# Gated scores and the state's part of the output as 64-row matmuls in the two halves of the array, both groups side by side

## The chip, the cores and the metric

The kernel runs on one core of a Trainium2 chip. TensorE multiplies matrices: a stationary operand is loaded into its array of 128 rows by 128 columns (a weight load, "PEld" in the profile), a moving operand streams past it (a matmul, "PE"), and the result goes to PSUM, eight banks of 512 fp32 numbers on each of 128 partitions. VectorE (DVE), ScalarE (ACT) and GpSimd (POOL) work element by element; SyncE (SP) issues most transfers. The metric is the device time of one execution in microseconds.

## What is computed

One decoder layer over 1024 rows of width 1024, in fp32. The part that the change touches is the gated linear attention: four heads, keys of 64, values of 128.

```python
b = jnp.cumsum(log_a, axis=-2)
qe = q * jnp.exp(b)
ke = k * jnp.exp(-b)
A = jnp.where(causal, jnp.einsum('bhncd,bhnsd->bhncs', qe, ke), 0.0)
o_intra = jnp.einsum('bhncs,bhnsv->bhncv', A, v)
# state of a chunk: S * decay + kd^T v, carried from chunk to chunk
o_inter = jnp.einsum('bhncd,bhndv->bhncv', qe, S_prev)
o = o_intra + o_inter
```

The output goes through a normalisation per head and a SiLU gate. Beside it runs a sliding-window softmax attention of eight query heads, then an output projection, and a convolutional gated MLP of width 2816, which takes most of the time.

## The kernel before

The 1024 rows are eight tiles (t = 0 to 7) of 128 rows. A dense unit multiplies one tile with one block of a weight matrix: eight steps over the depth, each in three passes of reduced-precision fp32 products (`dense`, line 317). The GLA phase takes the place of two 64-row chunks of the reference by one of 128 rows.

For each tile of the GLA:

- `unit_g` projects queries and keys (tile `dg`), and `gla_qk` multiplies them by the exponentials of the cumulated gate into `qe` and `kd`.
- `gla_tr` transposes both on TensorE into the bank `gt` (L560): four blocks, two for the queries and two for the keys. A block holds a pair of heads, the even head on partitions 0 to 63, the odd one on 64 to 127. ScalarE copies the keys into one tile (`gkt`, L565) and the queries into `qbd` (L563), a block-diagonal tile: for each pair two blocks of 128 columns, the first with the even head's rows and zeros below, the second with zeros above and the odd head's rows. The zeros are written once at the start (L517).
- `gla_a` (L591) multiplies, for each pair, all 128 key rows with the 256 columns of `qbd`. The zeros keep the two heads apart. The scores of four heads land in one bank `ga`; `copy_predicated` (L593) writes those on and below the diagonal into `asb`, which was zeroed at the start.
- `gla_o` adds up in one bank `go` the product of masked scores and values for each head (L600) and, from the second tile on, the product of the block of `qbd` with the state `s_mid` (L603). ScalarE squares the result (L606), VectorE sums the squares (L608) and copies the result over the values (L609).
- `gla_state` (L573, bank `cs`) makes the tile's contribution to the state, in two halves of 64 columns of the array; `gla_mid` (L586) and VectorE (L581) carry the state on in the two `s_mid` tiles in turn.

All of these products are of plain fp32 operands. `swa_pv` (L490, banks `pv`) of the window attention already uses array halves: first two column halves, then four quarters of 64 rows by 64 columns. A written order chains its matmuls.

The work is put down as a list of events with due times (`at(time, function, ...)`), sorted by time. Dense unit t of the queries and keys stands at TG + t; of tile t, `gla_tr` stands 1.0 later, `gla_mid` and `gla_state` at 1.75 and 1.8, `gla_a` at 1.9, `gla_o` at 2.7. A planner then orders each engine's instructions by its own model, and takes whatever is ready; only chained instructions keep their order. Transposes, decay products (`dec`, L538), cumulated gates (`bd`, L530) and the window attention's scores (`sc`), transposes (`ppt`) and outputs (`pv`) lie between the dense units.

Banks come from two pools of four in turn (`bank`): each request takes the bank that was given out eight requests earlier, once its readers are done. Small tiles of 2 KB a partition rotate through `K2` buffers (`k2_tile`).

Of the kernel before, what the change touches and what calls it, by code (L numbers as in the profile page):

```python
# [9 lines left out]
F32 = mybir.dt.float32  # L10
F32R = mybir.dt.float32r
I32 = mybir.dt.int32
AF = mybir.ActivationFunctionType
# [4 lines left out]
P = 128  # L18
# [12 lines left out]
HALF = (slice(0, 64), slice(64, 128))  # L31
# [3 lines left out]
def hymba_layer_kernel(ctx, tc, x, mix_norm, w_in, w_alpha2, b_alpha, gla_norm,  # L35
                       q_norm, k_norm, sinks, w_out, ffn_norm, w_up, conv_w,
                       conv_b, w_down, out):
    nc = tc.nc
    act, dve, pool, pe, sp = nc.scalar, nc.vector, nc.gpsimd, nc.tensor, nc.sync
# [15 lines left out]
    def bank(name):  # L55
        ps["n"] += 1
        if "f" in ps:
            return ps["f"][2 + ps["n"] % 2]

        for start, which in (("n2pt_6", "b"), ("do1_7", "a"), ("n2pt_3", "a")):  # L60
            if name.startswith(start):
                return ps[which].tile([P, 512], F32, tag="b", name=name)
        return ps["ab"[ps["n"] % 2]].tile([P, 512], F32, tag="b", name=name)

    big = base.tile([P, NT, KD, 2, P], F32R, name="big")

    RAW_BUFS, K4, K2, N_WARM = 3, 6, 5, 5

    def raw_tile(name):
        return base.tile([P, 1024], F32, tag="raw", name=name, bufs=RAW_BUFS)  # L70
# [33 lines left out]
    gl = sg.enter_context(tc.tile_pool(name="gl", bufs=1))  # L104
# [11 lines left out]
    amask = upper.bitcast(I32)  # L116
# [45 lines left out]
    def rms_scale(ss, n, w, name, p, tag, bufs=3):  # L162
        v = p.tile([P, w], F32, tag=tag + "v", name=name + "v", bufs=bufs)
        dve.tensor_scalar(v, ss, 1.0 / n, EPS, op0=ALU.mult, op1=ALU.add)
        r = p.tile([P, w], F32, tag=tag + "r", name=name + "r", bufs=bufs)
        pool.tensor_tensor(r, v, mhalf[:, :w], ALU.pow)
        return r
# [156 lines left out]
    kt = gl.tile([P, 2, T + P], F32R, name="kt")  # L324
# [24 lines left out]
    def k2_tile(name):  # L349
        return gl.tile([P, 512], F32, tag="k2", name=name, bufs=K2)  # L350
# [119 lines left out]
    def swa_pt(t, g):  # L470
# [10 lines left out]
            dve.tensor_sub(pt[:, 0], pb, pt[:, 1])  # L481
        pts[t, g] = pt

    def swa_pv(t):

        pbs = [bank(f"pv{t}_{i}")[:, 0:256].rearrange("p (j c) -> p j c", j=4) for i in range(2)]

        def part(g, b, rows, i, start, stop):
            rhs = pts[t, g][:, b, :].rearrange("p (j c) -> p j c", j=4)
            pe.matmul(pbs[i][HALF[g]], lhsT=vv[rows, t - 1 + b, HALF[g]], rhs=rhs[rows, :, HALF[i]],  # L490
                      start=start, stop=stop)
            ins = nc.cur_bb.bb.instructions[-1]
            if order:
                tc.add_manual_dep(ins, order[-1], mybir.DependencyInfo(
                    mybir.DependencyClass.NoSync, mybir.DependencyReason.DATA), reason="order of the program")
            order.append(ins.name)

        full, order = slice(0, P), []
        for i in range(2):
            for g in (1, 0):  # L500
                part(g, i if t else 1, full, i, True, t == 0)


        if t:
            for g in (1, 0):
                for i in range(2):
                    part(g, 1 - i, HALF[i], i, False, True)
        for i in range(2):
            act.copy(qo[:, t, :].rearrange("p (j c) -> p j c", j=4)[:, :, HALF[i]], pbs[i])
# [1 line left out]


    s_mid = [gl.tile([P, 2, P], F32, name=f"s_mid{i}") for i in range(2)]
    qbd = [gl.tile([P, 2, 2, P], F32, name=f"qbd{i}") for i in range(2)]
    asb = gl.tile([P, 4, P], F32, name="asb")
    for s in qbd + [asb]:
        pool.memset(s, 0.0)  # L517
    gkd, gdec, gfac, gex, gqk, gqt, glh, grs, vg = {}, {}, {}, {}, {}, {}, {}, {}, [None]

    def gla_lh(t):  # L520
        lh = k2_tile(f"lh{t}").bitcast(F32R).rearrange("p (r c) -> p r c", r=2)
# [34 lines left out]
    def gla_tr(t):  # L556
        pb = bank(f"gt{t}")
        for i in range(4):
            src = (gqk, gkd)[i // 2][t]
            pe.transpose(pb[:, i * P:(i + 1) * P], src[:, i % 2 * P:(i % 2 + 1) * P], ident)  # L560
        pv = pb.rearrange("p (i c) -> p i c", i=4)
        for lo in range(2):
            act.copy(qbd[t % 2][HALF[lo], :, lo, :], pv[HALF[lo], 0:2])  # L563
        kt = k2_tile(f"gkt{t}")[:, 0:256].rearrange("p (i c) -> p i c", i=2)
        act.copy(kt, pv[:, 2:4])  # L565
        gqt[t] = kt

    def gla_state(t):
        kd, v, fc, sm = gkd[t], vg[0][:, t, :], gfac[t + 1], s_mid[(t + 1) % 2]
# [14 lines left out]
    def gla_mid(t):  # L584
        for pr in range(2):
            act.activation(s_mid[t % 2][:, pr], s_mid[(t - 1) % 2][:, pr], AF.Copy, scale=gfac[t][:, pr:pr + 1])  # L586

    def gla_a(t):
        pb = bank(f"ga{t}")
        for pr in range(2):  # L590
            pe.matmul(pb[:, pr * 256:(pr + 1) * 256], lhsT=gqt[t][:, pr, :], rhs=qbd[t % 2][:, pr],  # L591
                      start=(pr == 0), stop=(pr == 1))
        dve.copy_predicated(asb, amask.rearrange("p (q c) -> p q c", q=1).broadcast_to((P, 4, P)),  # L593
                            pb.rearrange("p (q c) -> p q c", q=4))

    def gla_o(t):
        v = vg[0][:, t, :]
        pb = bank(f"go{t}")
        for h in range(4):
            pe.matmul(pb[:, h * P:(h + 1) * P], lhsT=asb[:, h, :], rhs=v[:, h * P:(h + 1) * P],  # L600
                      start=(h == 0), stop=(t == 0 and h == 3))
        for h in range(4 if t else 0):
            pe.matmul(pb[:, h * P:(h + 1) * P], lhsT=qbd[t % 2][:, h // 2, h % 2, :], rhs=s_mid[t % 2][:, h // 2, :],  # L603
                      start=False, stop=(h == 3))
        sq = k2_tile(f"gsq{t}")
        act.activation(sq, pb, AF.Square)  # L606
        ss = gl.tile([P, 4], F32, tag="gss", name=f"gss{t}", bufs=2)
        dve.tensor_reduce(ss, sq.rearrange("p (h d) -> p h d", d=P), op=ALU.add, axis=AX.X)  # L608
        dve.tensor_copy(v, pb)  # L609
        grs[t] = rms_scale(ss, P, 4, f"g{t}", gl, "gr", 8)  # L610

    def gate(t, pb):
# [7 lines left out]
    def gate_tr(t, gs):  # L620
        pb = bank(f"ogt{t}")
        for h in range(4):
            pe.transpose(pb[:, h * P:(h + 1) * P], gs[:, h * P:(h + 1) * P], ident)
        pv = pb.rearrange("p (h c) -> p h c", h=4)
        hi, lo = big[:, t, 0:4, 0, :], big[:, t, 0:4, 1, :]
        act.activation(hi, pv, AF.Copy, scale=glan)
        dve.scalar_tensor_tensor(lo, pv, glan, hi.bitcast(F32), op0=ALU.mult, op1=ALU.subtract)
        src = qo[:, t, :].rearrange("p (j c) -> p j c", j=4)
        hi, lo = big[:, t, 4:8, 0, :], big[:, t, 4:8, 1, :]
        split(src, hi, lo)  # L630
# [422 lines left out]
    def at(time, f, *a):  # L1053
        ev.append((time, len(ev), f, a))
# [34 lines left out]
    for c in halves:  # L1089
        split(mix_row[:, c], mix_hl[0][0:1, c], mix_hl[1][0:1, c], dve)  # L1090
        pb = bank(f"mix{len(mix_ps)}")
# [77 lines left out]
    for t in range(NT):  # L1169
        s = 11.0 + 1.9 * t  # L1170
        at(s - 0.3, swa_qt, t)
        at(s + 1.0, swa_scores, t, 0)
        at(s + 1.6, swa_scores, t, 1)
        at(s + 3.2, swa_pt, t, 0)
        at(s + 3.8, swa_pt, t, 1)
        at(s + 4.9, swa_pv, t)
        s = TG + t
        at(s - 2.4, gla_lh, t)
        at(s - 1.4, gla_exp, t)
        at(s + 1.0, gla_tr, t)  # L1180
        if t < NT - 1:
            if t:
                at(s + 1.75, gla_mid, t + 1)
            at(s + 1.8, gla_state, t)
        at(s + 1.9, gla_a, t)
        at(s + 2.7, gla_o, t)
        at(TR + t + 1.3, lambda tt=t: gate_tr(tt, psb.pop(("r", tt))))
    at(TO + 8.006, mark)
    at(TO - 0.05, open_acc)
# [9 lines left out]
    for n, (ch, name) in enumerate(LOW):  # L1199
# [6 lines left out]
    order = [(ch, i, name) for ch in range(NCH)  # L1206
             for i, name in enumerate({0: SEQ_FIRST, L: SEQ_LAST}.get(ch, SEQ)) if (ch, name) not in LOW]
# [96 lines left out]
```

## Time and profile before

| | |
|---|---|
| Time, median of 3 runs | 1055.09 us (1054.99 to 1056.57) |
| Profiled execution | 1055.06 us |
| Its span, first to last instruction | 1053.3 us |
| TensorE busy | 1046.6 us (99%) |
| VectorE, GpSimd, ScalarE busy | 801.7, 617.4, 480.2 us |
| Mean granted TensorE clock | 1.000 |

The page gives busy time by engine, the chain of work that ended last, and groups of instructions by line, engine and tile, with the count, the mean duration of one, and what ended the idle time before them. The chain can also be listed piece by piece for a stretch of time. A matmul's duration in the profile is its latency; matmuls overlap in the pipeline, so the pace is read from the chain's pieces. An fp32 product appears as two matmuls and two weight loads.

### The profile page before, as it was taken

The page shows a single profiled execution, that of the slowest core. Times are in us where ns is not written, and L with a number is a line of the kernel's source. Part 1 is how long each engine was busy: PE and PEld are TensorE (multiplying, and loading weights), DVE is VectorE, ACT ScalarE, POOL GpSimd, SP SyncE. Part 2 cuts the span into 40 slices and gives each one's busy share as a digit, 9 for nine tenths or more (in the row PEclk, how much of TensorE's full clock was granted, in tenths as well). Part 3 has the DMA queues.
Part 4 walks back from the last instruction along what each step waited for, and adds up shares of the span by engine and source line. Part 5 has one row for each costly group of instructions (what it writes and reads, how often), then busy time and mean ns, then how long its engine had stood idle before and what let it go on. Part 6 is the DMA issues. An engine that isn't in the chain of part 4 may idle for free.

```text
span 1053.3 us, 13923 instructions
## 1 busy us (share of the span) xinstructions
PE 1046.6 (99%) x4976; PEld 850.7 (81%) x4976; DVE 801.7 (76%) x1332; ACT 480.2 (46%) x988; POOL 617.4 (59%) x510
## 2 busy tenths in 40 slices
PE   9999999999999999999999999999999999999998
PEld 6898877888888888888888888888888888888887
DVE  6776667754131699787979898897979798897986
ACT  5627654444340446554444445444444444444441
POOL 4592132325450205867868687877778687978750
PEclk9999999999999999999999999999999999999999
DMA  6152113002043202112121111112121211122104
GB/s 214 60 152 61 44 49 93 21 1 81 1 126 154 60 1 80 40 41 81 40 80 34 48 51 49 60 61 61 40 80 40 61 40 44 57 61 60 41 21 159
DMA packets 67502, 67.13 MB, mean 64 GB/s; under 512 B 4648, under 2 KB 52201, under 8 KB 67434
## 3 DMA queue, kind: packets, MB, share of 16 engines
q1 hardware_dynamic: 63448, 61.27, 18.8%
q10 hardware_dynamic: 3986, 4.99, 2.0%
q8 instruction: 39, 0.64, 0.3%
q14 instruction: 29, 0.24, 0.1%
HBM read 57.33 MB, written 4.19 MB: 58 GB/s over the span
## 4 chain that ended last, share of the span: by engine, by line
PE 98%; DMA 1%; ACT 0%; DVE 0%; issue 0%; POOL 0%; DVEq 0%; ACTq 0%
PE fb L834 39%; PE dn_P L1015 18%; PE do L317 9%; PE dv L317 4%; PE dr L317 4%; PE dg L317 4%; PE dq L317 3%; PE dk L317 2%; PE gb L834 2%; PE dq L707 1%; PE pv L490 1%; PE dl L1044 1%; PE fb L1044 1%; PE sc L443 1%; PE sc L442 1%; PE go L600 1%
## 5 line engine op out<-in xcount | busy, mean ns | idle before, releaser
L1019 DVE TENSOR_TENSOR acc<-acc,dn_P 128x1024 f32<-128x1024 f32 x140 | 169.8, 1214 | 63.6 <-PE dn_P L1015 63.4
L1015 PE MATMUL dn_P<-dw,dg 128*128 128x512 f32 x840 | 215.8, 393 | 0.0
L1015 PEld LDWEIGHTS dn_P<-dw,dg 128*128 128x128 f32 x840 | 157.7, 188 | 37.1
L317 PE MATMUL do<-wow,big 128*128 128x512 f32 x384 | 92.9, 398 | 0.0
L95 POOL TENSOR_TENSOR dw<-dn,dw 128x512 fp32r<-128x512 f32 x50 | 69.1, 1381 | 26.0 <-PE dn_P L1015 22.3
L317 PEld LDWEIGHTS do<-wow,big 128*128 128x128 f32 x384 | 71.1, 188 | 16.3
L886 ACT COPY ca<-fb 128x512 f32<-128x512 f32 x62 | 36.3, 585 | 72.2 <-PE fb L834 72.1
L834 PE MATMUL fb<-big,A11w 128*128 128x512 f32 x252 | 63.0, 396 | 0.0
L834 PE MATMUL fb<-big,S1w 128*128 128x512 f32 x252 | 62.9, 396 | 0.0
L834 PE MATMUL fb<-big,S4w 128*128 128x512 f32 x252 | 62.9, 396 | 0.0
L834 PE MATMUL fb<-ex,S2w 128*128 128x512 f32 x252 | 62.8, 397 | 0.0
L834 PE MATMUL fb<-ex,S3w 128*128 128x512 f32 x252 | 62.8, 396 | 0.0
L834 PE MATMUL fb<-big,A12w 128*128 128x512 f32 x252 | 62.5, 396 | 0.0
L834 PE MATMUL fb<-ex,A22w 128*128 128x512 f32 x252 | 62.5, 397 | 0.0
L841 DVE SCALAR_TENSOR_TENSOR ua<-fb,cc,ua 128x511 f32<-128x511 f32 x84 | 62.1, 740 | 0.3
L834 PEld LDWEIGHTS fb<-big,S1w 128*128 128x128 f32 x252 | 47.4, 188 | 11.6
L834 PEld LDWEIGHTS fb<-big,A11w 128*128 128x128 f32 x252 | 47.4, 188 | 11.6
L834 PEld LDWEIGHTS fb<-big,S4w 128*128 128x128 f32 x252 | 47.4, 188 | 11.6
L834 PEld LDWEIGHTS fb<-ex,S2w 128*128 128x128 f32 x252 | 47.4, 188 | 11.4
L834 PEld LDWEIGHTS fb<-ex,S3w 128*128 128x128 f32 x252 | 47.4, 188 | 11.4
L834 PEld LDWEIGHTS fb<-ex,A22w 128*128 128x128 f32 x252 | 47.4, 188 | 11.4
L834 PEld LDWEIGHTS fb<-big,A12w 128*128 128x128 f32 x252 | 47.3, 188 | 11.1
(432 smaller groups left out, 2404.3 us busy)
## 6 DMA issues: line engine op xcount, KB each, us to landing
up<-in_w_up_dram SPq DMA_DIRECT2D x44, 512.0 KB, 3.8
dn<-in_w_down_dram SPq DMA_DIRECT2D x22, 512.0 KB, 3.5
acc<-in_x_dram SPq DMA_DIRECT2D x8, 512.0 KB, 6.5
out_dram<-acc SPq DMA_DIRECT2D x15, 256.0 KB, 2.0
xt<-in_x_dram SPq DMA_DIRECT2D x7, 512.0 KB, 3.3
vraw<-in_w_in_dram SPq DMA_DIRECT2D x4, 512.0 KB, 3.9
graw<-in_w_in_dram SPq DMA_DIRECT2D x4, 512.0 KB, 3.6
qt<-qt ACTq DMA_DIRECT2D x16, 128.0 KB, 2.2
```

The source lines that it names most:

```text
L95: (eng or pool).tensor_sub(lo, src, hi.bitcast(F32))
L317: pe.matmul(pb[:, :n], lhsT=big[:, t, k, ra, :], rhs=ws[k][:, rb, :n], start=(k == 0 and i == 0), stop=(k == KD - 1 and i == 2))
L442: pe.matmul(pbs[-1][:, j % 2, :], lhsT=q[:, g, qc], rhs=kt[:, g, kc], start=True, stop=False)
L443: pe.matmul(pbs[-1][:, j % 2, :], lhsT=ql[:, g, qc], rhs=kt[:, g, kc], start=False, stop=True)
L490: pe.matmul(pbs[i][HALF[g]], lhsT=vv[rows, t - 1 + b, HALF[g]], rhs=rhs[rows, :, HALF[i]], start=start, stop=stop)
L600: pe.matmul(pb[:, h * P:(h + 1) * P], lhsT=asb[:, h, :], rhs=v[:, h * P:(h + 1) * P], start=(h == 0), stop=(t == 0 and h == 3))
L834: pe.matmul(pb, lhsT=w[:, ra, k, :], rhs=b_operand(bn, k, rb), start=(onto is None and i == 0), stop=(i == 11), skip_group_check=onto is n ...
L841: dve.scalar_tensor_tensor(dst, src, w, dst, op0=ALU.mult, op1=ALU.add)
L886: act.copy(dst, pb)
L1015: pe.matmul(pb[:, i], lhsT=g[:, ra, c:c + P], rhs=w[:, rb, :], start=(onto is None and n == 0), stop=(n == 2), skip_group_check=onto is no ...
L1019: dve.tensor_add(acc, acc, pb)
L1044: pe.matmul(pb[:, c0:c1], lhsT=g[:, ra, (t % 4) * P:(t % 4 + 1) * P], rhs=w[:, rb, c0:c1], start=(ch == NCH - 2 and i == 0), stop=(ch == N ...
```

## The change

The block-diagonal tiles `qbd` go. `gla_tr` copies the whole transposed bank, queries and keys, into one small tile. Scores are four products of 64 rows, one for each head, with that head's half of the partitions as operands; even and odd heads write different banks. The state's part is four products of 64 rows in the same manner, and comes ahead of the intra-chunk part in the two banks. A chain fixes the order of all of these products through all tiles: scores of tile t, then state's part and intra-chunk part of tile t - 1. The mask becomes a step of its own behind the state's update, and mask, square and copy become two instructions each, one for each bank. `K2` goes from 5 to 7. The chaining code of `swa_pv` becomes the helper `chain`.

```diff
-    RAW_BUFS, K4, K2, N_WARM = 3, 6, 5, 5
+    RAW_BUFS, K4, K2, N_WARM = 3, 6, 7, 5
...
+    def chain(order):
+        ins = nc.cur_bb.bb.instructions[-1]
+        if order:
+            tc.add_manual_dep(ins, order[-1], mybir.DependencyInfo(
+                mybir.DependencyClass.NoSync, mybir.DependencyReason.DATA), reason="order of the program")
+        order.append(ins.name)
+
+    g_order = []
...
-    qbd = [gl.tile([P, 2, 2, P], F32, name=f"qbd{i}") for i in range(2)]
     asb = gl.tile([P, 4, P], F32, name="asb")
-    for s in qbd + [asb]:
-        pool.memset(s, 0.0)
+    pool.memset(asb, 0.0)
...
-        pv = pb.rearrange("p (i c) -> p i c", i=4)
-        for lo in range(2):
-            act.copy(qbd[t % 2][HALF[lo], :, lo, :], pv[HALF[lo], 0:2])
-        kt = k2_tile(f"gkt{t}")[:, 0:256].rearrange("p (i c) -> p i c", i=2)
-        act.copy(kt, pv[:, 2:4])
-        gqt[t] = kt
+        qt = gqt[t] = k2_tile(f"gqt{t}").rearrange("p (i c) -> p i c", i=4)
+        act.copy(qt, pb.rearrange("p (i c) -> p i c", i=4))
...
     def gla_a(t):
-        pb = bank(f"ga{t}")
+        qt = gqt[t]
+        pbs = [bank(f"ga{t}_{lo}") for lo in range(2)]
         for pr in range(2):
-            pe.matmul(pb[:, pr * 256:(pr + 1) * 256], lhsT=gqt[t][:, pr, :], rhs=qbd[t % 2][:, pr],
-                      start=(pr == 0), stop=(pr == 1))
-        dve.copy_predicated(asb, amask.rearrange("p (q c) -> p q c", q=1).broadcast_to((P, 4, P)),
-                            pb.rearrange("p (q c) -> p q c", q=4))
+            for lo in range(2):
+                pe.matmul(pbs[lo][:, pr * P:(pr + 1) * P], lhsT=qt[HALF[lo], 2 + pr, :], rhs=qt[HALF[lo], pr, :],
+                          start=(pr == 0), stop=(pr == 1))
+                chain(g_order)
+        gas[t] = pbs
+
+    def gla_mask(t):
+        for lo in range(2):
+            dve.copy_predicated(asb.rearrange("p (a b) c -> p b a c", a=2)[:, lo],
+                                amask.rearrange("p (q c) -> p q c", q=1).broadcast_to((P, 2, P)),
+                                gas[t][lo][:, 0:256].rearrange("p (q c) -> p q c", q=2))
 
     def gla_o(t):
-        v = vg[0][:, t, :]
-        pb = bank(f"go{t}")
-        for h in range(4):
-            pe.matmul(pb[:, h * P:(h + 1) * P], lhsT=asb[:, h, :], rhs=v[:, h * P:(h + 1) * P],
-                      start=(h == 0), stop=(t == 0 and h == 3))
-        for h in range(4 if t else 0):
-            pe.matmul(pb[:, h * P:(h + 1) * P], lhsT=qbd[t % 2][:, h // 2, h % 2, :], rhs=s_mid[t % 2][:, h // 2, :],
-                      start=False, stop=(h == 3))
+        v, qt = vg[0][:, t, :], gqt[t]
+        pbs = [bank(f"go{t}_{lo}") for lo in range(2)]
+        for pr in range(2 if t else 0):
+            for lo in range(2):
+                pe.matmul(pbs[lo][:, pr * P:(pr + 1) * P], lhsT=qt[HALF[lo], pr, :], rhs=s_mid[t % 2][HALF[lo], pr, :],
+                          start=(pr == 0), stop=False)
+                chain(g_order)
+        for pr in range(2):
+            for lo in range(2):
+                h = pr * 2 + lo
+                pe.matmul(pbs[lo][:, pr * P:(pr + 1) * P], lhsT=asb[:, h, :], rhs=v[:, h * P:(h + 1) * P],
+                          start=(t == 0 and pr == 0), stop=(pr == 1))
+                chain(g_order)
...
+        at(s + 1.9, gla_a, t)
+        if t:
+            at(s + 1.91, gla_o, t - 1)
         if t < NT - 1:
             if t:
-                at(s + 1.75, gla_mid, t + 1)
-            at(s + 1.8, gla_state, t)
-        at(s + 1.9, gla_a, t)
-        at(s + 2.7, gla_o, t)
+                at(s + 1.93, gla_mid, t + 1)
+            at(s + 1.94, gla_state, t)
+        else:
+            at(s + 2.7, gla_o, t)
+        at(s + 1.95, gla_mask, t)
```

More of the change, by code (lines that the diff above doesn't have):

```diff
@@ L491, in part @@
                       start=start, stop=stop)
[L492 to L496, printed above, removed]
+            chain(order)
         full, order = slice(0, P), []
@@ L513, in hymba_layer_kernel @@
     s_mid = [gl.tile([P, 2, P], F32, name=f"s_mid{i}") for i in range(2)]
-    qbd = [gl.tile([P, 2, 2, P], F32, name=f"qbd{i}") for i in range(2)]
     asb = gl.tile([P, 4, P], F32, name="asb")
-    for s in qbd + [asb]:
-        pool.memset(s, 0.0)
-    gkd, gdec, gfac, gex, gqk, gqt, glh, grs, vg = {}, {}, {}, {}, {}, {}, {}, {}, [None]
+    pool.memset(asb, 0.0)
+    gas, gkd, gdec, gfac, gex, gqk, gqt, glh, grs, vg = {}, {}, {}, {}, {}, {}, {}, {}, {}, [None]
     def gla_lh(t):
@@ L605, in gla_o @@
         sq = k2_tile(f"gsq{t}")
-        act.activation(sq, pb, AF.Square)
+        for lo in range(2):
+            act.activation(sq.rearrange("p (a b c) -> p b a c", a=2, b=2)[:, lo],
+                           pbs[lo][:, 0:256].rearrange("p (a c) -> p a c", a=2), AF.Square)
         ss = gl.tile([P, 4], F32, tag="gss", name=f"gss{t}", bufs=2)
         dve.tensor_reduce(ss, sq.rearrange("p (h d) -> p h d", d=P), op=ALU.add, axis=AX.X)
-        dve.tensor_copy(v, pb)
+        for lo in range(2):
+            dve.tensor_copy(v.rearrange("p (a b c) -> p b a c", a=2, b=2)[:, lo],
+                            pbs[lo][:, 0:256].rearrange("p (a c) -> p a c", a=2))
```

## The prediction

> **What bounds the kernel now.** I read the page first, then the waits of TensorE, then busy time by stretch, then the chain of work for the stretch in which the gated linear attention (GLA) runs. Page of the kernel before:
>
> ```profile
> span 1053.3 us, 13923 instructions
> PE 1046.6 (99%) x4976; PEld 850.7 (81%) x4976; DVE 801.7 (76%) x1332; ACT 480.2 (46%) x988; POOL 617.4 (59%) x510
> PE 98%; DMA 1%; ACT 0%; DVE 0%; issue 0%; POOL 0%; DVEq 0%; ACTq 0%
> ```
>
> The chain that ends last is TensorE for 98%. The waits of TensorE, first for 150 to 290 us, then for 270 us to the end, and the busy time from 170 to 270 us (columns: stretch, its length, then each engine's busy us and instructions, granted clock, DMA share, GB/s):
>
> ```profile
> PE sc L443 <- DMA ql<-ql: 0.7, 1, 0.7
> PE gb L834 <- ACT big L255: 0.2, 1, 0.2
> 170.00:270.00 100.00, 100.00 (x634) 82.56 (x633) 58.85 (x162) 45.40 (x141) 35.72 (x33) 1.00 0.12 33
> ```
>
> In the stretch that the change touches TensorE is busy 100.00 of 100 us, it waits once before it and 0.2 us after it, and no other engine is above 59%. So a TensorE microsecond taken out here should come off the end, and work on the other engines costs nothing while it finds room. "Busy" hides the pace, though; that stands in the chain, where each piece is TensorE's own time (start us, length us, line, count of passes):
>
> ```profile
> 200.33 0.89 PE go L600 x8
> 201.22 0.89 PE go L603 x8
> ...
> 204.44 0.86 PE ga L591 x4
> ...
> 212.00 0.67 PE go L600 x6
> 212.67 0.34 PE dec L538 x4
> 213.01 0.33 PE go L600 x2
> ...
> 224.86 0.45 PE go L603 x4
> 225.31 0.34 PE dec L538 x4
> 225.65 0.55 PE go L603 x4
> 226.20 0.59 PE cs L573 x8
> 226.79 1.06 PE ga L591 x4
> 227.85 5.60 PE dg L317 x24
> 233.45 0.44 PE gt L560 x4
> ...
> 255.46 1.61 PE pv L490 x16
> 257.07 1.09 PE go L600 x8
> ```
>
> **Paces.** An fp32 product is two passes here, each with its weight load. One pass of 256 columns (ga) takes 0.86/4 = 0.215 us, one of 128 columns (go) 0.89/8 = 0.111 us, a transpose 0.44/4 = 0.11 us. How often each runs, by shape (array rows*columns, then the result):
>
> ```profile
> L600 PE MATMUL go<-vg,asb 128*128 128x128 f32 x64 | 8.9, 279 | 0.0
> L591 PE MATMUL ga<-qbd,gkt 128*128 128x256 f32 x32 | 8.5, 388 | 0.0
> L603 PE MATMUL go<-s_mid,qbd 128*128 128x128 f32 x56 | 7.6, 276 | 0.0
> L573 PE MATMUL cs<-vg,kd 128*64 128x128 f32 x56 | 4.6, 285 | 0.0
> L490 PE MATMUL pv<-pt,vv 64*64 64x256 f32 x48 | 4.0, 402 | 0.0
> ```
>
> The scores (L591) are four passes in each of 8 chunks, the state's part (L603) eight in each of 7, the intra-chunk part (L600) eight in each of 8. The last stays.
>
> **What side-by-side products cost.** The state product cs runs in column halves (128*64): eight passes in 0.59 us, where 4 pairs at 0.11 us would be 0.44 us. So the halves do run together, and entering and leaving that shape costs 0.15 us inside the piece. The piece behind pays more: ga takes 1.06 instead of 0.86 us behind cs, go L600 1.09 instead of 0.89 us behind pv, 0.20 us each. One excursion out of the full array and back therefore costs 0.35 us. Row halves, which the change uses, appear in pv's second half (the timeline of TensorE and of its weight loads; then the loads of that form over 182 to 272 us):
>
> ```profile
> 188.42 0.66 PE L490 MATMUL pv<-pt,vv 64*64 64x256 f32 x8
> 188.42 0.21 PEld L490 LDWEIGHTS pv<-pt,vv 64*64 64x64 f32 x8 [0.39 <-issue]
> L490 PEld LDWEIGHTS pv<-pt,vv 64*64 64x64 f32 x32 | 0.8, 131 | 1.5 <-issue 1.5
> ```
>
> Eight passes of 256 columns end after 0.66 us; one behind the other they would take 8 x 0.215 = 1.72 us. Two row halves and two column halves work at once, writing two banks, and the eight weight loads of 0.13 us all begin within 0.21 - 0.13 = 0.08 us.
>
> **The change, part by part.**
>
> Scores of a chunk: two full products of 256 columns, half of them zeros, become four of 64 rows and 128 columns, in pairs over the two row halves. 4 x 0.215 = 0.86 us become 4 pairs. No row shows 64 rows by 128 columns. Bounds for a pair: 0.111 us, one pass of go, if the halves run together, and 0.222 us, two passes, if they don't. I take 0.111, because pv shows the row halves together and go shows that 128-column weights keep that pace. So 0.44 us, plus the excursion.
>
> State's part: eight passes of 128 columns stay eight passes, but pair up: 0.89 us become 4 x 0.111 = 0.44 us.
>
> Both side by side: scores of chunk t and state's part of chunk t-1 are chained in one order, so they can share one excursion. Its price: 0.35 us from cs and pv; bounds 0 (if a row split needs no draining) and 0.70 us (double, since twice as many weight columns must be loaded before the pace is regained). I take 0.35.
>
> The sum, against the profiled execution:
>
> - t = 2 to 7, six shared excursions: before 0.86 + 0.89 = 1.75 us, after 0.89 + 0.35 = 1.24 us, gain 0.51 each, 3.06 us.
> - scores of t = 0 and 1, alone (chunk 0 has no state's part): 0.86 against 0.44 + 0.35 = 0.79, gain 0.07 each, 0.14 us.
> - state's part of chunk 7, alone: 0.89 against 0.79, gain 0.10 us.
> - together 3.30 us.
> - One break. The planner may put other work inside a run: dec stands inside L600 at 212.67 and inside L603 at 225.31, two of 15 go runs. Between row-split passes that costs another 0.35 us. I count one: gain 2.95 us.
>
> The profiled execution took 1055.06 us, 1.76 us beyond its span, and the median of the runs is 1055.09 us, so nothing need be shifted: 1055.06 - 2.95 = **1052.1 us**.
>
> Work off the path. Groups of ScalarE and VectorE from 160 to 272 us, and of GpSimd at the start:
>
> ```profile
> L563 ACT COPY qbd<-gt 64x256 f32<-64x256 f32 x16 | 5.8, 365 | 17.8 <-PE gt L560 17.7
> L606 ACT ACTIVATE gsq<-go 128x512 f32<-128x512 f32 x8 | 4.7, 589 | 1.6 <-PE go L600 0.8 <-PE go L603 0.7
> L509 ACT COPY qo<-pv 128x256 f32<-128x256 f32 x10 | 3.2, 377 | 4.2 <-PE pv L490 4.2
> L565 ACT COPY gkt<-gt 128x256 f32<-128x256 f32 x8 | 3.0, 373 | 0.2
> L593 DVE COPY_PREDICATED asb<-upper,ga 128x512 f32<-128x512 int32 x8 | 5.9, 740 | 1.9 <-PE ga L591 1.9
> L609 DVE COPY vg<-go 128x512 f32<-128x512 f32 x8 | 5.4, 681 | 0.0
> L554 DVE SCALAR_TENSOR_TENSOR kd<-dg,rn,ex 128x256 f32<-128x256 f32 x8 | 3.8, 475 | 0.0
> 6.22 1.28 POOL L295 TENSOR_TENSOR qw<-qraw,qw 128x512 fp32r<-128x512 f32 x1 [2.53 <-ACT qw L291]
> ```
>
> Per chunk ScalarE loses 2 x 0.365 + 0.373 = 1.10 us of copies and gets one of 128x512, about 0.59 by the square's row; the square becomes two of about 0.377, +0.17. VectorE's mask and copy become two each; at 0.475 (the 128x256 row) that is 1.90 against 1.42 us, +0.48 at most. Eight chunks add under 4 us to an engine with 41 us idle in this stretch; each is covered by the next dense unit (dg, 5.60 us). Without that cover it would cost 0.48 us a chunk. The two memsets of qbd go from GpSimd's start, where it then waits 2.53 us for ScalarE: worth nothing. Two more k2 buffers replace qbd's 4 KB; the transposed q and k live in one until the state's part is done, and of the seven the next to reuse theirs is chunk t+3's qe, which is written later anyway.
>
> The order: the state's part of t-1 now waits for the scores of t by the written chain; if their copy is late, the dense unit fills in and the block moves behind it. gla_mid and gla_state come behind the block, and the mask behind those, so in VectorE's queue the mask stands behind the reduction and copy of t-1 and the state's two updates. Late next is the masked score matrix, which is not read until the next block, a unit on. No DMA is issued by any moved step.
>
> **The rivals.**
>
> *The pieces fall apart.* Scores and state's part meet in no chunk, because their four banks are not free together. Each of six blocks then pays a second 0.35 us: 3.30 - 2.10 = 1.2 us gain, 1053.9 us. For: the two dec pieces above, and scores placed alone inside a dense unit at 204.44. Against: both operands are ready long before, and the written order puts the products next to each other.
>
> *The halves do not overlap* (slower). The weights of a half are loaded only when its running matmul has ended, or the two halves load one after the other: a pair takes 0.222 us. A block is 8 x 0.222 + 0.35 = 2.13 against 1.75, +0.38 six times; scores alone 0.89 + 0.35 = 1.24 against 0.86, +0.38 twice; the last state's part 1.24 against 0.89, +0.35: +3.4 us, 1058.5 us. It decides from a pair of (1.75 - 0.35)/8 = 0.175 us on. Against: the eight 64*64 loads begin within 0.08 us, while the first matmuls of the same rows run. For: those had 64 weight columns, and here are 128. The Trainium skill, "TensorE: Matmul & The Clock Gate", Part 3 (What overlaps and what doesn't), says that a weight load overlaps a running matmul only where its row group differs; by that the alternating halves would wait as in this rival, and pv's loads do not agree with it.
>
> *Banks.* A chunk takes four PSUM banks for scores and output instead of two, of eight in rotation, and the scores keep theirs until the late mask. If TensorE has nothing else to run it stands as at the one wait above, 0.7 us, in chunks 1 to 4 where sliding-window work competes: 2.8 us lost, 1055.0 us. Against: no such wait in the 100 us now, and dense units to fill.
>
> *The split drains nothing.* 0.35 us fewer on nine excursions and the break: 1055.06 - 3.30 - 3.15 = 1048.6 us. Against: every change of shape in the chain is paid for.
>
> **How the numbers follow.** Forecast 0.60 (1050.8 to 1053.0: switches of 0.30 to 0.45 us, up to two breaks); falling apart 0.20; banks 0.08; no overlap 0.07; no draining 0.05. The range of 1050.3 to 1055.3 us holds the first three and leaves out the last two and the edges of the others, about 0.15 in all. A measurement tells 0.2%, 2.1 us, from no change. Faster: the forecast, no draining and a little of the second, 0.67; within 0.2%: the rest of that and most of banks, 0.23; slower: no overlap and the worst of banks, 0.10.
>
> **What would show it.** In the chain after: ga as eight passes in about 0.45 to 0.60 us and the state's part as eight right behind it without another shape between; go L600 behind them at 1.09 instead of 0.89 us; cs and dense units unchanged. Pairs of passes 0.11 us apart mean overlap, 0.22 the slower rival. New pieces between the two mean the second. TensorE waits for VectorE or ScalarE in 170 to 270 us mean banks. The prediction is wrong if a row-split block costs above 1.75 us, or if the order elsewhere changes by more than 2 us.

## The result and the profile after

The changed kernel takes 1056.78 us (median of 21 runs, 1055.73 to 1059.05) against 1055.06 us (21 runs of before on the same chips). The ratio is 1.0015, with a 95% interval of 1.0009 to 1.0022: slower by some 1.7 us, which lies inside the 0.2% (2.1 us) that the forecast took as no change. The forecast was 1052.1 us and a range of 1050.3 to 1055.3. Both the range and the sign were missed. A second round of eleven runs gave 1056.89 against 1055.05 us, ratio 1.0012 (1.0003 to 1.0020). In some executions of most kernels here, before included, the mean granted TensorE clock is 0.998 or less in place of 1.000, and these take some 1.7 to 3.5 us longer than the others of the same kernel (last section).

The page of the changed kernel, the three lines that answer to those of before:

```profile
span 1056.3 us, 13999 instructions
PE 1046.2 (99%) x5008; PEld 847.0 (80%) x5008; DVE 799.7 (76%) x1348; ACT 476.2 (45%) x980; POOL 615.8 (58%) x508
PE 96%; DVE 1%; DMA 1%; ACT 1%; issue 1%; POOL 0%; ACTq 0%; DVEq 0%; SPq 0%
```

TensorE's share of the chain fell from 98 to 96%, and VectorE, ScalarE and "issue" (time in which the engine waited for nothing that the profile shows) came in: new waits. This execution also ran 3.4 us at half the TensorE clock, in front of the part that was changed (last section), so all that follows is read from a profile of the same kernel in the second round (1056.96 us, clock 1.000). TensorE's waits there, from 100 to 290 us; before had the one on `ql` (a tile of the window attention's queries that arrives by a transfer) alone, 0.7 us:

```profile
PE ga L594 <- ACT gqt L566: 1.9, 2, 1.0
PE sc L443 <- DMA ql<-ql: 1.0, 1, 1.0
PE go L610 <- DVE sm L450: 0.6, 1, 0.6
PE dg L317 <- DVE asb L601: 0.3, 1, 0.3
```

And its chain of work, piece by piece (scores L594, state's part L610, intra-chunk part L616):

```profile
169.41 5.61 PE dg L317 x24
...
176.72 0.42 PE ga L594 x2
...
178.01 0.59 PE cs L573 x8
178.59 0.64 PE ga L594 x6
...
201.83 0.72 PE go L610 x8
...
214.24 0.65 PE ga L594 x8
214.89 0.45 PE go L610 x8
215.33 1.09 PE go L616 x8
216.42 0.59 PE cs L573 x8
...
224.81 0.41 PE ga L594 x2
...
225.76 0.53 PE ga L594 x5
...
247.42 0.72 PE ga L594 x8
...
259.01 0.78 PE ga L594 x8
...
274.70 0.44 PE ogt L641 x4
```

The piece at 214 us (chunk 3) is the forecast's picture. Scores and state's part stand side by side, 0.65 + 0.45 us, and the intra-chunk part behind them takes 1.09 us, 0.20 more than alone. Eight passes without entry take 0.45 us, that is 0.11 us a pair: the two halves work at once. With the entry of 0.20 us and the exit of 0.20 us a shared excursion costs 0.40 us, where 0.35 was taken; the block costs 1.30 us against 1.75 before. So the products gained what they should, nearly. The chain of before has the same two ends at these times:

```profile
169.27 5.61 PE dg L317 x24
...
273.34 0.44 PE ogt L623 x4
```

From the second dense unit to these transposes before took 273.34 - 169.27 = 104.07 us, the changed kernel 274.70 - 169.41 = 105.29 us, 1.22 us more. This stretch holds all of the changed products and none of the disturbance at the transfer of `ql`, and several experiments below are measured on it too.

**Why the scores wait.** ScalarE's timeline of the changed kernel around the copies of chunks 6 and 7 (start, length, line, then in brackets the idle time before and what ended it):

```profile
245.75 1.14 ACT L92 CAST rw<-rraw 128x512 fp32r<-128x512 f32 x2 [1.66 <-DMA rraw<-in_w_in_dram]
246.79 0.58 ACT L566 COPY gqt<-gt 128x512 f32<-128x512 f32 x1
...
256.50 1.28 ACT L632 ACT_TABLE_LOAD   x1
257.79 0.69 ACT L632 ACTIVATE gs<-dr,rn 128x512 f32<-128x512 f32 x1
258.38 0.58 ACT L566 COPY gqt<-gt 128x512 f32<-128x512 f32 x1
```

TensorE's timeline ahead of the scores of chunk 6:

```profile
245.80 0.60 PE L475 MATMUL ppt<-ident,pr 128*128 128x128 f32 x4
247.42 0.72 PE L594 MATMUL ga<-gqt 64*128 64x128 f32 x8 [1.03 <-ACT gqt L566]
```

ScalarE's queue stands 1.66 us for the transfer of the gate's weights, then casts two of them, and only then copies the transposed q and k. TensorE is ready for the scores at 245.80 + 0.44 = 246.24 us and starts them at 247.42. At chunk 7 the copy stands behind a table load of 1.28 us and the gate's activation. In the kernel before the copies of chunk 6 were as late; ScalarE there:

```profile
245.33 1.14 ACT L92 CAST rw<-rraw 128x512 fp32r<-128x512 f32 x2 [1.66 <-DMA rraw<-in_w_in_dram]
246.38 0.74 ACT L563 COPY qbd<-gt 64x256 f32<-64x256 f32 x2
247.13 0.37 ACT L565 COPY gkt<-gt 128x256 f32<-128x256 f32 x1
```

and TensorE:

```profile
246.83 0.94 PE L603 MATMUL go<-s_mid,qbd 128*128 128x128 f32 x7
247.71 0.66 PE L573 MATMUL cs<-vg,kd 128*64 128x128 f32 x8
248.29 1.43 PE L317 MATMUL dr<-rw,big 128*128 128x512 f32 x5
249.56 1.02 PE L591 MATMUL ga<-qbd,gkt 128*128 128x256 f32 x4
```

They end at 247.50, and the scores begin at 249.56, 2.06 us later: output of the chunk before, state update and five dense passes stood in between. The change took 0.5 us off the copies and put the scores in front of all of that. In the kernel before, the copies of chunk 7 end at 258.46 and its scores begin at 259.12, 0.66 us later. The planner fixes TensorE's order before the run by its own idea of when a copy is done; on the chip nothing fills in.

**The account** on the stretch. The forecast's gain of 2.95 us; nine excursions at 0.40 instead of 0.35 us, +0.45; two breaks (chunk 0 at 176.72, chunk 4 at 224.81) at 0.40 instead of one at 0.35, +0.45. The four waits, from the time at which TensorE was ready to the time at which it started (246.24 to 247.42 above), are 1.18 and 0.98 for the copies of chunks 6 and 7, 0.63 at the state's part behind the scores of chunk 2, for a bank that the softmax holds, and 0.44 at a dense unit behind the mask, +3.23. Together +1.18; measured +1.22. So close a fit is partly luck: the wait at chunk 2 parts scores and state's part, and the latter then takes 0.72 us instead of 0.45 (201.83), which is not counted. Of the rest, the profiled executions show 0.14 us ahead of the stretch (169.41 against 169.27), where the wait on `ql` is longer, and 0.3 us behind it; its cause I have not assigned.

### The profile page after: what moved, and what is told of

Read it like the earlier page. It is cut to its first block, busy times and chain, and to the rows that moved or that the text cites. A ratio compares the mean times of both kernels' runs of the same rounds, so it can differ in the third digit from the quotient of the medians.

```text
span 1056.3 us, 13999 instructions
## 1 busy us (share of the span) xinstructions
PE 1046.2 (99%) x5008; PEld 847.0 (80%) x5008; DVE 799.7 (76%) x1348; ACT 476.2 (45%) x980; POOL 615.8 (58%) x508
## 4 chain that ended last, share of the span: by engine, by line
PE 96%; DVE 1%; DMA 1%; ACT 1%; issue 1%; POOL 0%; ACTq 0%; DVEq 0%; SPq 0%
PE fb L852 39%; PE dn_P L1033 18%; PE do L317 8%; PE dv L317 4%; PE dr L317 4%; PE dg L317 3%; PE dq L317 3%; PE dk L317 2%; PE gb L852 2%; PE dq L725 1%; PE pv L500 1%; PE dl L1062 1%; PE fb L1062 1%; PE sc L443 1%; PE go L616 1%; PE sc L442 1%
## 5 line engine op out<-in xcount | busy, mean ns | idle before, releaser
L466 POOL TENSOR_TENSOR pr<-pr,sm 128x512 f32<-128x512 f32 x16 | 17.2, 1073 | 73.8 <-DVE sm L465 29.1
```

The costliest lines, as they stand in the source:

```text
L466: pool.tensor_tensor(pr, pr, den[:, hs].rearrange("p (j o) -> p j o", o=1).broadcast_to((P, 4, P)), ALU.mult)
```

## The experiments

Theory A: the products gain what was forecast, and the waits in the new order eat it. Theory B: the row-split products themselves cost more. Times are medians, with ratios against runs of before made beside them: 1055.28 us for the first four experiments, 1054.90 for the two excursions, both remedies, the whole block later and the casts, 1055.05 for the two blocks later and the second rounds.

**The new products in the old order.**

```diff
-        at(s + 1.9, gla_a, t)
-        if t:
-            at(s + 1.91, gla_o, t - 1)
         if t < NT - 1:
             if t:
-                at(s + 1.93, gla_mid, t + 1)
-            at(s + 1.94, gla_state, t)
-        else:
-            at(s + 2.7, gla_o, t)
+                at(s + 1.75, gla_mid, t + 1)
+            at(s + 1.8, gla_state, t)
+        at(s + 1.9, gla_a, t)
         at(s + 1.95, gla_mask, t)
+        at(s + 2.7, gla_o, t)
```

> The 64-row products as changed, but the steps in the order of before: state update, scores, mask, and the output of a chunk behind the scores of the same chunk; scores and the state's part of the output each pay their own excursion. Theory A (the products gain what was forecast, and the loss comes from TensorE standing in front of the scores for ScalarE's late copy, 2.2 us in the changed kernel's trace, and for banks and the mask, about 1 us): the scores stand 2.1 us later than in the changed kernel, the copy is there, waits of TensorE on the copy fall to below 0.5 us; fifteen excursions of 0.35 us and four breaks of the planner leave a gain of about 1.3 - 1.4 = 0 us: 1055.1 us, 1054.3 to 1055.8. Theory B (the row-split products cost more than the full ones, order is no matter): slower than the changed kernel's 1056.8, since there are more excursions, 1058 us or more.

Measured 1055.89 us, ratio 1.0012 (1.0002 to 1.0021). The only wait of TensorE left from 100 to 290 us is that on `ql`, 0.8 us. The stretch is 1.02 us longer than before. By the account it should be 1.15 us longer: the products themselves win 6.45 us (3.30 us and nine excursions at 0.35 given back), and fifteen excursions and four breaks at 0.40 us cost 7.60. The median lies 0.1 us above Theory A's range of 1054.3 to 1055.8, and far below the 1058 us of B.

**The old products in the new order.**

```diff
-        for h in range(4):
-            pe.matmul(pb[:, h * P:(h + 1) * P], lhsT=asb[:, h, :], rhs=v[:, h * P:(h + 1) * P],
-                      start=(h == 0), stop=(t == 0 and h == 3))
         for h in range(4 if t else 0):
             pe.matmul(pb[:, h * P:(h + 1) * P], lhsT=qbd[t % 2][:, h // 2, h % 2, :], rhs=s_mid[t % 2][:, h // 2, :],
-                      start=False, stop=(h == 3))
+                      start=(h == 0), stop=False)
+            chain(g_order)
+        for h in range(4):
+            pe.matmul(pb[:, h * P:(h + 1) * P], lhsT=asb[:, h, :], rhs=v[:, h * P:(h + 1) * P],
+                      start=(t == 0 and h == 0), stop=(h == 3))
+            chain(g_order)
...
-        at(s + 1.9, gla_a, t)
-        at(s + 2.7, gla_o, t)
+        at(s + 1.9, gla_a, t)
+        if t:
+            at(s + 1.91, gla_o, t - 1)
...
```

The edit is against the kernel before. Beyond these lines the scores are chained too, the mask is a step of its own, and it and the state's update have the times of the changed kernel.

> The full-array products of before with the block-diagonal queries, but in the order of the changed kernel (scores of t, then state's part and intra-chunk part of t - 1 in one chain, mask as its own step). Theory A: the waits for the copies remain or grow (three copies of 1.10 us instead of one of 0.57), and the 3.3 us of the side-by-side products are missing: 1058.5 to 1061 us. Theory B: as fast as the changed kernel or faster, 1055 to 1057 us.

Measured 1061.23 us, ratio 1.0060 (1.0046 to 1.0073). Only five executions were made, and four of them, 1061.00 to 1061.63 us, have the mean clock of 0.998; the one at 1.000, which is the profiled one, took 1058.83 us. So some 2.4 us of the median go with the lower clock. The scores among TensorE's groups, 170 to 271 us:

```profile
L600 PE MATMUL ga<-qbd,gkt 128*128 128x256 f32 x32 | 8.8, 398 | 3.3 <-ACT gkt L574 3.3
```

The stretch takes 277.15 - 168.74 = 108.41 us, 4.34 more than before, 3.3 of them idle at the scores of chunks 6 and 7. The changed kernel's is 1.22 us longer than before, so the products of the change win 3.1 us back; about half a microsecond of that is less waiting (2.8 us idle in all there). All five executions lie above B's 1055 to 1057 us: the products are faster, and the order is what loses.

**The intra-chunk part first.**

```diff
-        for pr in range(2 if t else 0):
...
         for pr in range(2):
             for lo in range(2):
                 h = pr * 2 + lo
                 pe.matmul(pbs[lo][:, pr * P:(pr + 1) * P], lhsT=asb[:, h, :], rhs=v[:, h * P:(h + 1) * P],
-                          start=(t == 0 and pr == 0), stop=(pr == 1))
+                          start=(pr == 0), stop=(t == 0 and pr == 1))
                 chain(g_order)
+        for pr in range(2 if t else 0):
+            for lo in range(2):
+                pe.matmul(pbs[lo][:, pr * P:(pr + 1) * P], lhsT=qt[HALF[lo], pr, :], rhs=s_mid[t % 2][HALF[lo], pr, :],
+                          start=False, stop=(pr == 1))
+                chain(g_order)
...
-        at(s + 1.9, gla_a, t)
         if t:
-            at(s + 1.91, gla_o, t - 1)
+            at(s + 1.9, gla_o, t - 1)
+        at(s + 1.91, gla_a, t)
```

> The changed kernel with the chain turned round: intra-chunk part of t - 1, state's part of t - 1, then the scores of t, still side by side with the state's part. The scores come 1.3 us later behind the same transposes. Theory A: most of the two waits for the copy (1.2 and 1.0 us) is covered, 1056.8 - 2.0 = 1054.8 us, 1054.0 to 1055.3; those for banks and mask may stay. Theory B: no change, 1056.5 to 1057.2 us.

> The run with the intra-chunk part first once more, on the same chip as the others of this call: 1053.6 us and faster than before by about 1.4 us if that result holds; 1055 us if it was chance.

Measured 1053.62 us, ratio 0.9987 (0.9976 to 0.9997; one of its eleven executions took 2650.9 us, for no reason that I know), and in the second round 1053.05 us, ratio 0.9978 (0.9967 to 0.9989). TensorE in the second, around chunk 6:

```profile
244.09 0.60 PE L475 MATMUL ppt<-ident,pr 128*128 128x128 f32 x4
244.53 1.06 PE L611 MATMUL go<-vg,asb 128*128 128x128 f32 x8
245.51 0.71 PE L616 MATMUL go<-s_mid,gqt 64*128 64x128 f32 x8
246.06 0.69 PE L594 MATMUL ga<-gqt 64*128 64x128 f32 x8
```

and ScalarE:

```profile
245.40 0.58 ACT L566 COPY gqt<-gt 128x512 f32<-128x512 f32 x1
```

The copy ends at 245.98 and the scores begin at 246.06. The same copy, no earlier against its transposes, is now just covered by the sixteen passes in front; the waits on banks and the mask are gone too, which is why the run is faster than Theory A's 1054.0 to 1055.3 us. The ends of the stretch:

```profile
168.97 5.61 PE dg L317 x24
...
270.92 0.44 PE ogt L641 x4
```

It takes 101.95 us, 2.12 less than before. By the account it should be 3.30 - 0.45 - 2 x 0.40 = 2.05 less, with two breaks here too. Same products, same number of excursions, another order: that is the forecast's gain at the measured price of nine excursions and two breaks, and it puts 3.2 and 3.8 us between this run and the changed kernel's medians.

**The copy earlier.**

```diff
-        at(s + 1.0, gla_tr, t)
+        at(s + 0.92, gla_tr, t)
```

> The changed kernel with the transposes of a chunk and their copy put down ahead of the next dense unit instead of behind it; the copy is issued up to one unit (5.6 us) earlier. Theory A: TensorE no longer waits for the copy anywhere, 1056.8 - 2.2 = 1054.6 us, 1053.5 to 1055.2. Theory B: no change, 1056.5 to 1057.2 us.

Measured 1054.01 us, ratio 0.9989 (0.9980 to 0.9998). No wait on the copy is left; that of 0.7 us at the state's part for a bank that the softmax holds stays. Either cover, work in front or an earlier copy, gives the gain back or most of it, so it is the waits in the new order that lose, those on the copy above all. Neither run prices the copy alone, since the wait behind the mask went with it in both; the run with the casts, below, does so for chunk 6.

**Two excursions for one.**

```diff
-        at(s + 1.9, gla_a, t)
         if t:
-            at(s + 1.91, gla_o, t - 1)
+            at(s + 1.9, gla_o, t - 1)
+        at(s + 1.91, gla_a, t)
```

> As the run with the intra-chunk part first, but in the order state's part, intra-chunk part, scores: the intra-chunk part now stands between the two row-split groups, so that each of six chunks has two excursions instead of one; the scores come as late as there. If an excursion costs 0.35 us as the forecast took it, 6 x 0.35 = 2.1 us slower than that run's 1053.6: 1055.7 us, and 0.35 more if the planner breaks one run. If sharing is worth nothing: 1053.6 us.

Measured 1055.77 us, 2.15 us above the first run with the intra-chunk part first. Its chain at chunk 5:

```profile
237.31 0.65 PE go L610 x8
237.96 1.09 PE go L616 x8
239.04 0.65 PE ga L594 x8
```

Both groups now pay their entry (0.65 instead of 0.45 us), and the intra-chunk part between them pays the exit (1.09). Six more excursions were put at 2.1 us; having them side by side is worth about what was forecast, or a little more: this stretch is 2.50 us longer than in the second run with the intra-chunk part first, with three breaks against two. Without the sharing the change gains nothing (1055.77 us against 1054.90 before).

**Both remedies.** Edit: those of the intra-chunk part first and of the copy earlier together.

> Intra-chunk part first and the transposes with their copy put down ahead of the next dense unit. If the late copy was the only loss and each of the two covers it alone, nothing more is gained: 1053.6 us, 1053.0 to 1054.2. If some of it was still left in the run with the intra-chunk part first: 1052.5 to 1053.0.

Measured 1054.58 us, ratio 1.0001 (0.9992 to 1.0010). Nothing is added; some 1 us of the gain of the run with the intra-chunk part first is lost. TensorE's longest wait:

```profile
PE sc L442 <- DVE pt L481: 0.9, 1, 0.9
```

The planner arranged the phase anew, and the window attention's scores now wait for a bank that VectorE holds. I had expected 1054.2 us at worst. That the wait accounts for the whole loss is not shown.

**The whole block later.** Edit: in the run with the intra-chunk part first, 0.2 is added to the times of `gla_o`, `gla_a`, `gla_mid`, `gla_state` and `gla_mask` (not to the last `gla_o`).

> Intra-chunk part first, and the whole block (output of t - 1, scores of t, state update, mask) put down 0.2 of a unit later, behind the next dense unit and the next transposes in the list. The planner then leaves the scores of chunks 0 and 1 in one piece, where two breaks of 0.35 us stood: 1053.6 - 0.7 = 1052.9 us, if breaks cost what was forecast; 1053.6 if they cost nothing; above 1054 if the later block runs into banks or the softmax.

Measured 1054.55 us, ratio 1.0001 (0.9992 to 1.0010). The breaks are gone, but the waits are back, in other places:

```profile
PE go L611 <- DVE asb L601: 1.3, 1, 1.3
PE dr L317 <- DVE vg L626: 0.7, 1, 0.7
```

The first is at the last chunk, at 267.12: its `gla_o` was not moved, so that the mask stands 0.2 of a unit nearer to it. The second is at 247.34, where a dense unit finds its bank still held by a result that VectorE has not copied.

**Two blocks later.** Edit: the 0.2 for chunks 0 and 1 alone.

> Intra-chunk part first, and only the blocks of chunks 0 and 1 put down 0.2 of a unit later. In TensorE's program both breaks are gone and no other block moves into the softmax's way. If a break costs 0.4 us, as an excursion measured in the traces: 0.8 us faster than the intra-chunk part first (1053.6): 1052.8 us. If the run that moved all blocks lost time for the move itself and not for waits on VectorE in the later chunks: 1053.6 us or slower.

Measured 1053.4 us, ratio 0.9980 (0.9970 to 0.9989); beside it the intra-chunk part first had 1053.05. In TensorE's chain the scores of chunks 0 and 1 stand in one piece each, at 182.66 and 194.77. Its timeline behind the scores of chunk 2:

```profile
201.73 0.66 PE L573 MATMUL cs<-vg,kd 128*64 128x128 f32 x8 [0.77 <-DVE ql L430]
```

Two breaks were saved and a wait of 0.77 us came in, for the bank of the state update. That the median did not move doesn't price the breaks; this run leaves their 0.4 us open.

**The casts on the other engine.**

```diff
-        at(TR - 0.9 + d, load_piece, "r", CR, 512, i, (None, dve))
+        at(TR - 0.9 + d, load_piece, "r", CR, 512, i, (None, dve), dve)
```

> The changed kernel with the eight casts of the gate's weight block moved from ScalarE to VectorE, so that ScalarE's queue no longer holds casts that wait for the transfer of these weights ahead of the copy of q and k for chunk 6. If that queue is the cause, TensorE's wait of 1.2 us at the scores of chunk 6 goes and the one of 1.0 us at chunk 7 (behind the gate's activation) stays: 1056.8 - 1.2 = 1055.6 us. If the copy is late for another reason: 1056.8 us or slower.

Measured 1056.69 us, as slow as the changed kernel. TensorE's order is the same; at chunk 6:

```profile
248.80 0.72 PE L594 MATMUL ga<-gqt 64*128 64x128 f32 x8 [0.29 <-ACT gqt L566]
```

The wait fell from 1.03 to 0.29 us, so ScalarE's queue behind the weights' transfer was the cause of most of it at chunk 6, and the one at chunk 7 stayed at 0.9. The ends of the stretch:

```profile
171.54 5.60 PE dg L317 x24
...
276.08 0.44 PE ogt L641 x4
```

It takes 104.54 us, 0.75 less than in the changed kernel, as much as the wait fell by. In the order of the changed kernel, then, the wait on the copy comes off the time of the stretch one for one. But the median did not follow. The profiled execution is the slowest of the eleven, 1058.97 us, with a stretch at half clock and 4.6 us from its last matmul to its end, where the other twelve profiles have 3.5; whether the other ten lost their time there too is not known.

**The changed kernel once more**, for the profile read above.

> The changed kernel once more, on the same chip as the others of this call: 1056.8 us, about 1.7 us slower than before and 3.1 us slower than with the intra-chunk part first, in its trace again TensorE's waits of about 1.0 us at the scores of chunks 6 and 7.

Measured 1056.89 us; the two waits at chunks 6 and 7 are there at 1.03 and 0.91 us.

## Why the prediction was wrong

- *Pace of a pair, 0.111 us; halves together.* Right: 0.45 us for eight passes at 214.89. The bounds were 0.111 and 0.222 us, and the lower one held. The rival in which the halves do not overlap is out. The Trainium skill ("TensorE: Matmul & The Clock Gate", Part 3, What overlaps and what doesn't) says that a weight load overlaps a running product only where its row group differs; the trace doesn't agree. The weight loads of the changed kernel, 170 to 272 us:

```profile
L594 PEld LDWEIGHTS ga<-gqt 64*128 64x128 f32 x64 | 4.8, 186 | 3.7 <-ACT gqt L566 2.6 <-issue 0.6 <-ACT qo L515 0.2
```

  A load takes 0.186 us and pairs follow each other every 0.11 us, so the loads of a half run while that half multiplies.
- *Price of an excursion, 0.35 us.* Near: 0.40. The entry costs 0.20 us inside the piece, where the 64-column products cost 0.15. Nine of them, 0.45 us. With prices of 0.30 to 0.45 us and up to two breaks the sum gives 1051.3 to 1053.6 us, not the 1050.8 to 1053.0 of the forecast.
- *One break.* Two, 0.45 us more with their price. The pieces did not fall apart: scores and state's part follow each other in five of six blocks, and in the sixth a wait parts them.
- *Work off the path: "each is covered by the next dense unit".* This is the step that failed, together with "if their copy is late, the dense unit fills in and the block moves behind it". I counted ScalarE's and VectorE's work in sums of busy time and found room. What decided was when one copy is done: I did not look up how far the scores of before stood behind their copies (2.06 us at chunk 6, 0.66 at chunk 7), nor what lies ahead of the copy in ScalarE's queue there (a wait of 1.66 us for a transfer). TensorE's program is fixed before the run, and nothing filled in. The waits on the copy cost 2.2 us, a term that the sum put at nothing.
- *Banks.* A rival with a chance of 0.08, at 2.8 us (1054.9 us by its own sum, not 1055.0). It was there in part: 0.63 us for a bank that the softmax held, 0.44 us where the next dense unit waited behind the mask. "No such wait in the 100 us now" was weak evidence, since the order was about to change.
- *The profile's first reading*, TensorE busy for 100 of 100 us, was right and misled: it says that nothing waits in this order, not that there is slack for another.
- *The chances.* 0.10 on slower, and that on overlap and banks. No rival had the new order itself as its mechanism, though the part on the order named the wait.

## What to carry to other kernels

When a step moves to the front on a saturated engine, measure its operand's margin in the old profile, from the end of the last producer to the start of the reader, and what stands ahead of that producer in its queue; the busy shares do not show it. Put independent work ahead of the reader before shortening the producer: turning the chain round made the same products 3.2 to 3.8 us faster. Group the products that use array halves, since each excursion into row halves costs 0.40 us here, nearly as much as eight passes of 128 columns in pairs (0.45).

## What the runs showed of the hardware

Three of the thirteen profiles show TensorE's granted clock at 0.50 for 3.4 us, beginning 0.3 to 1.4 us behind the end of its wait on `ql`. That wait is 1.33 us long in two of them and 1.24 in the third (the casts on the other engine); in the ten profiles without such a stretch it is 0.54 to 1.17 us. The first profile of the changed kernel:

```profile
165.71 0.39 PE L443 MATMUL sc<-kt,ql 128*128 128x256 f32 x1 [1.33 <-DMA ql<-ql]
...
167.06 2.77 PE L500 MATMUL pv<-pt,vv 128*64 128x256 f32 x16
```

and its busy time by stretch (stretch, length, busy us and instructions of TensorE, its weight loads, VectorE, ScalarE and GpSimd, then granted clock):

```profile
163.00:166.00 3.00, 1.67 (x12) 1.41 (x11) 2.60 (x9) 2.47 (x12) 0.81 (x2) 1.00 0.55 148
166.00:169.40 3.40, 3.40 (x18) 1.90 (x21) 0.00 (x0) 0.00 (x0) 0.95 (x1) 0.50 0.00 0
```

With a wait of 1.0 us at the same place, 1.98 us busy in the same 3 us, the second profile kept the clock at 1.00 and finished the window attention's output as fast as before. That the wait is the cause is inferred from these thirteen profiles; no run set its length. The Trainium skill ("TensorE: Matmul & The Clock Gate", Part 1, HAM oscillation) advises against idle gaps beyond about 3.4 us; here the clock fell behind gaps of 1.24 and 1.33 us. The stretch at half clock lies ahead of the changed products and is not part of the account.
